# A two-layer hybrid decoder trunk whose opening is written in another order: x loaded first, squares summed in threes, bias indicators off GpSimd

## The chip, the core and the metric

The kernel runs on one core of a Trainium2 chip. Time is device time in microseconds (us) of one execution; the time of a kernel is the median of its runs. The core's engines each work through their own queue in order: TensorE (PE in the profile; its weight loads are PEld), VectorE (DVE), ScalarE (ACT) and GpSimd (POOL). Nearly all transfers are issued from SyncE's queue (SP), also in order.

## The reference

Two layers (DEPTH 2) over 512 tokens of width 2048. Each layer has a modulated RMS norm, one input projection into 7504 columns, sparse attention with an index scorer (top 128 keys, a T5 relative-position bias shared by both layers), retention with rotary, and one output projection:

```python
for l in range(DEPTH):
    mod = c_act @ w_mod[l] + b_mod[l]
    shift, scale, gate = jnp.split(mod, 3, axis=-1)
    h = rmsnorm(x, norm_gain[l]) * (1.0 + scale[:, None, :]) + shift[:, None, :]
    proj = h @ w_in[l]
    q_a, k_a, v_a, g_a, q_i, k_i, w_i, q_b, k_b, v_b, g_b = jnp.split(proj, split_points, axis=-1)
    q_a = rmsnorm(q_a.reshape(B, S, N_HEADS_A, HEAD_DIM), q_norm_gain[l])
    k_a = rmsnorm(k_a, k_norm_gain[l])
    att = sparse_attention(q_a, k_a, v_a, q_i.reshape(B, S, IDX_HEADS, IDX_DIM), k_i, w_i,
                           positions, rel_bias)
    y_a = att.reshape(B, S, D_A) * jax.nn.silu(g_a)
    q_b = rotary(q_b.reshape(B, S, N_HEADS_B, HEAD_DIM), positions)
    k_b = rotary(k_b.reshape(B, S, N_HEADS_B, HEAD_DIM), positions) * (HEAD_DIM ** -0.5)
    ret = retention(q_b, k_b, v_b.reshape(B, S, N_HEADS_B, HEAD_DIM))
    y_b = head_groupnorm(ret, ret_norm_gain[l]).astype(x.dtype) * jax.nn.silu(g_b)
    y = jnp.concatenate([y_a, y_b], axis=-1) @ w_out[l]
    x = x + gate[:, None, :] * y
```

The bias is `rel_bias[t5_bucket(pos_q - pos_k)]`, a table lookup per query, key and head; it does not depend on the layer's data.

## The kernel before, in words

Everything is held with features on the partitions: x and the normalised input h are 16 K-tiles of 128 features by 512 tokens. A projection is a product of fp32 numbers that are split into an upper and a lower fp32r half, so that each product is three matmuls (lines 330 to 332, or 336 to 338 for groups that are laid out by token): h upper with w upper, h lower with w upper, h upper with w lower. For the weights ScalarE writes the upper half (`wh`, line 268) and VectorE the lower (`wl`, line 275), each into a ring of three buffers; the loaded chunk `wf` has a ring of three too. `ahead` issues loads, upper and lower halves a chunk or two before the chunk's matmuls.

Work is a `stream` of chunks of groups. A group owns some columns of w_in, a few PSUM tiles and a function that evacuates them; a chunk is two to four K-tiles of it.

The opening, `start()`, is recorded by hand: each engine's queue has the instructions in the order in which Python issues them. It does five things.

1. It loads x and squares it on ScalarE; VectorE adds the squares, PE sums them over partitions (`row_sums`, line 511, tile `prs`), and `rstd_col` makes 1/rms and broadcasts it through PE (`prb`, line 493). `warm(n)` (line 476, tile `pw`) puts n small matmuls of zeros into PE's queue, whose result nobody reads.
2. It computes layer 0's modulation. Each K-tile needs a shift and a scale column, each one VectorE instruction over a 128 x 2048 piece of w_mod (1 MB) times the broadcast silu(c) (`mod_add`, line 357; the first four columns are done in two halves). In the text they are the adds. A K-tile of h then takes x times rstd (line 527, VectorE), the upper half (line 533, ScalarE), the same in fp32 (line 537 on ScalarE, or 535 on VectorE for the first tiles), and the lower half (line 539, VectorE).
3. Since K-tiles come one by one, PE is given early work, in the order of `PLAN`. `("S", c)` is chunk c (K-tiles 2c and 2c+1) of the group S, which holds the attention keys, values and index keys; `("S", 0, k)` is one K-tile of chunk 0. `("E", i, a, b)` is K-tiles a to b-1 of piece i, over 256 columns; pieces 0 to 3 are index queries (QI, 384 tokens), 4 to 7 are one retention head's query and key each (QB and KB, 512 tokens). A fourth number again means one K-tile alone. The result of a first piece is copied out by ScalarE (`part`, line 1257); later pieces of the same columns are added to it by VectorE (line 1272). The groups behind the opening start where PLAN stopped (`EARLY`) and join the stored part (line 1264).
4. The loop over `WORK` (PLAN with costs) decides how the rest is woven in: after each item its cost is added to `t`, and when `t` reaches RMOD one more add is issued (`mod_step`); if an item needs a K-tile that has not been issued, adds are forced first. In the same way a bias unit is issued for each RBIAS of cost, once KBIAS K-tiles are there.
5. The bias tables: 32 units. Each has four indicator tiles (positions against thresholds) and twelve bf16 matmuls with 32 columns of stationary operand (line 790, tile `pb`), a copy out of PSUM with an added column (`bt`, line 797) and a store to DRAM. Indicators are 0.5/-0.5 values by GpSimd (line 779, with doubled tables `be`) or signs by ScalarE (line 781). Seven units (`EU`, five of them on GpSimd) are issued by hand; `bias_tables` issues the rest, in the loop and then in the steady part.

PSUM has two tags of four banks: `pj` for S and all later groups, `px` for the early pieces E, the bias units, `warm` and the steady part's small products.

Behind the opening, `step` takes the stream chunk by chunk and `fill` runs tasks (index scores, top-k, rotary, retention, attention, bias) beside it; there the order is a scheduler's.

The lines that order the opening before:

```python
for k in range(KT):
    q = G("sq") if k else ssq
    act(q, X[k], AF.Square)
    ...
    if k % 3 == 0 and 0 < k < KT - 1:
        col = row_sums(pss, q, col)
        warm(WS if k < 12 else WL)
    elif k:
        tt(ssq, ssq, q, op=OP.add)
    if k < 3:
        mod0_add()
```

Of the kernel before, what the change touches and what calls it, by code (L numbers as in the profile page):

```python
# [45 lines left out]
PLAN = [("S", 0, 0), ("E", 0, 0, 2, 0), ("S", 0, 1), ("E", 0, 0, 2, 1), ("E", 1, 0, 2),  # L46
# [7 lines left out]
RBIAS, KBIAS = 6.0, 3  # L54
# [81 lines left out]
def hybrid_trunk(ctx, tc, xt, positions, wmod, w_in, w_out, cst_d, dec_d, out):  # L136
# [343 lines left out]
    def rstd_col(pss, n, then=None, tag="px"):  # L480
# [4 lines left out]
        if then:  # L485
            then()
        nc.vector.reciprocal(r, r)
# [55 lines left out]
    def start():  # L543
        rot, bias = rot_tables(), bias_tables()
        mod0_loads(4)
        for k in range(KT):
            load_x(k)
        ahead(1, 0)
        mod0_loads(6)
        ahead(2, 0)  # L550
# [32 lines left out]
        ssq, col, u = G("ssq"), 0, 0
        mod0_add()
        for k in range(KT):
            q = G("sq") if k else ssq
            act(q, X[k], AF.Square)
# [774 lines left out]
```

## Time and profile before

| | us |
|---|---|
| median of 3 runs (lowest, highest) | 1901.75 (1899.94, 1902.48) |
| the profiled execution, its own time | 1902.44 |
| its span | 1900.6 |
| PE busy, PEld busy | 1857.5, 1557.3 |
| DVE, ACT, POOL busy | 1300.0, 802.0, 90.6 |
| mean granted PE clock | 0.986 |

The profile is one execution. Matmuls are pipelined, so a busy PE is not PE at its peak; what counts is where it starts late or waits. The span is cut into 40 slices of 47.5 us for the overview; finer stretches come from the trace. A wait in brackets names the engine whose instruction ended it. Differences between kernels are taken from the profiled execution's own time (1902.44, of which 1900.6 is the span) and then applied to the median.

### The profile page before, as it was taken

The numbers are of one execution on the slowest core, as the hardware profiler recorded it, in microseconds if no ns is written. First come the engines' busy times: TensorE is split into PE (matmuls) and PEld (weight loads), VectorE is DVE, ScalarE is ACT, GpSimd is POOL, SyncE is SP. The second block draws the span as 40 slices with busy tenths as digits, with TensorE's granted clock in tenths as the row PEclk, the third lists the DMA queues.
The fourth block names the chain that finished last, engine by engine and source line by source line (L and its number), as shares of the span: only waits on it lengthen the run. The fifth ranks groups of instructions, "written<-read, shape, count | busy, mean of one in ns | idle before, by whom it ended". The sixth has DMA issues, their size and how long they took to land.

```text
span 1900.6 us, 24723 instructions
## 1 busy us (share of the span) xinstructions
PE 1857.5 (98%) x9124; PEld 1557.3 (82%) x9124; DVE 1300.0 (68%) x2254; ACT 802.0 (42%) x1480; POOL 90.6 (5%) x172
## 2 busy tenths in 40 slices
PE   6899999999999999999999999999999999999999
PEld 5687888888888888888889987888888888888887
DVE  7688599898767855777767689466775785564232
ACT  5665572355446532322225441245444554233211
POOL 8200000000000000100000000000000000000000
PEclk6899999999999999999999999999999999999999
DMA  9789423333353546789873333333334254653442
GB/s 341 283 301 294 132 60 89 100 111 105 99 183 114 178 143 202 241 268 309 293 258 105 101 87 97 108 95 100 105 102 131 74 189 133 189 180 119 144 142 102
DMA packets 166617, 304.43 MB, mean 160 GB/s; under 512 B 16352, under 2 KB 72416, under 8 KB 162912
## 3 DMA queue, kind: packets, MB, share of 16 engines
q1 hardware_dynamic: 166208, 302.37, 49.8%
q8 instruction: 71, 1.16, 0.2%
q10 hardware_dynamic: 288, 0.48, 0.1%
q14 instruction: 50, 0.41, 0.1%
HBM read 289.18 MB, written 13.63 MB: 159 GB/s over the span
## 4 chain that ended last, share of the span: by engine, by line
PE 82%; DVE 9%; ACT 4%; issue 2%; POOL 2%; DMA 2%; SPq 0%; DVEq 0%; ACTq 0%
PE pj L332 19%; PE pj L330 19%; PE pj L331 19%; PE pj L336 5%; PE pj L338 5%; PE pj L337 5%; DVE wl L275 2%; DVE mw L357 2%; POOL ind L779 2%; DVE iacc L928 1%; DVE m L927 1%; DVE iacc L913 1%; DMA xT<-in_xt_dram 1%; PE ptr L173 1%; ACT qsq L1075 1%
## 5 line engine op out<-in xcount | busy, mean ns | idle before, releaser
L275 DVE TENSOR_TENSOR wl<-wf,wh 128x1024 fp32r<-128x1024 f32 (+2 forms) x309 | 366.0, 1185 | 438.8 <-ACT wh L268 427.0
L268 ACT ACTIVATE wh<-wf 128x1024 fp32r<-128x1024 f32 (+2 forms) x309 | 318.8, 1032 | 794.0 <-PE pj L331 567.7
L332 PE MATMUL pj<-h,wl 128*128 128x512 f32 (+1 forms) x1280 | 486.1, 380 | 4.3 <-DVE wl L275 4.3
L330 PE MATMUL pj<-h,wh 128*128 128x512 f32 (+1 forms) x1280 | 488.1, 381 | 0.7 <-DVE join L1264 0.7
L331 PE MATMUL pj<-h,wh 128*128 128x512 f32 (+1 forms) x1280 | 486.0, 380 | 0.4 <-DVE h L539 0.4
L332 PEld LDWEIGHTS pj<-h,wl 128*128 128x128 f32 x1280 | 240.4, 188 | 46.0 <-DVE wl L275 5.7
L330 PEld LDWEIGHTS pj<-h,wh 128*128 128x128 f32 x1280 | 240.5, 188 | 44.7 <-issue 3.5
L331 PEld LDWEIGHTS pj<-h,wh 128*128 128x128 f32 x1280 | 240.4, 188 | 39.8 <-DVE h L539 0.9
L336 PE MATMUL pj<-wh,h 128*128 128x512 f32 (+1 forms) x640 | 242.5, 380 | 2.6 <-DVE vm L943 2.5
L338 PE MATMUL pj<-wh,h 128*128 128x512 f32 (+1 forms) x640 | 240.8, 378 | 1.6 <-DVE h L539 1.6
L337 PE MATMUL pj<-wl,h 128*128 128x512 f32 (+1 forms) x640 | 241.8, 378 | 0.0
L332 PE MATMUL pj<-y,wl 128*128 128x512 f32 x512 | 199.3, 389 | 0.0
L331 PE MATMUL pj<-y,wh 128*128 128x512 f32 x512 | 199.3, 389 | 0.0
L330 PE MATMUL pj<-y,wh 128*128 128x512 f32 x512 | 199.3, 389 | 0.0
L336 PEld LDWEIGHTS pj<-wh,h 128*128 128x128 f32 x640 | 121.6, 190 | 25.9 <-ACT wh L268 3.3
L338 PEld LDWEIGHTS pj<-wh,h 128*128 128x128 f32 x640 | 121.2, 190 | 21.8 <-DVE h L539 1.8
L337 PEld LDWEIGHTS pj<-wl,h 128*128 128x128 f32 x640 | 121.6, 190 | 19.4 <-DVE wl L275 0.2
L330 PEld LDWEIGHTS pj<-y,wh 128*128 128x128 f32 x512 | 96.1, 188 | 20.2
L331 PEld LDWEIGHTS pj<-y,wh 128*128 128x128 f32 x512 | 96.1, 188 | 19.9
L332 PEld LDWEIGHTS pj<-y,wl 128*128 128x128 f32 x512 | 96.1, 188 | 19.8
L357 DVE CUSTOM_DVE_ANT_0 mw<-mw,cb 128x1024 f32<-128x1024 f32 (+1 forms) x64 | 93.0, 1453 | 7.3 <-POOL mp L356 5.6
L357 DVE CUSTOM_DVE_ANT_0 mw<-mw,cb,mp 128x1024 f32<-128x1024 f32 x68 | 89.2, 1311 | 12.6 <-POOL md L356 7.6
(442 smaller groups left out, 2167.5 us busy)
## 6 DMA issues: line engine op xcount, KB each, us to landing
wf<-in_w_in_dram SPq DMA_DIRECT2D x155, 512.0 KB, 3.6
mw<-in_wmod_dram SPq DMA_DIRECT2D x136, 512.0 KB, 5.7
wf<-in_w_in_dram SPq DMA_DIRECT2D x136, 256.0 KB, 3.1
wf<-in_w_out_dram SPq DMA_DIRECT2D x64, 512.0 KB, 4.1
mw<-in_wmod_dram SPq DMA_DIRECT2D x28, 1024.0 KB, 7.8
dec<-in_decay_dram SPq DMA_DIRECT2D x32, 256.0 KB, 4.1
xT<-in_xt_dram SPq DMA_DIRECT2D x16, 256.0 KB, 5.4
bias<-bias_d SPq DMA_DIRECT2D x16, 256.0 KB, 4.1
```

Of the source, the lines that this page charges most:

```text
L173: nc.tensor.transpose(o, i, idn)
L268: act(h[:, :n], wf[i][:, :n], AF.Copy)
L275: tt(lo[:, :n], wf.pop(i)[:, :n], f(whl[i][:, :n]), op=OP.subtract)
L330: mm(q, wh[:, o:o + P], ah, start=s0, stop=False)
L331: mm(q, wh[:, o:o + P], al, start=False, stop=False)
L332: mm(q, wl[:, o:o + P], ah, start=False, stop=s1)
L336: mm(q, ah[:, n * P:(n + 1) * P], wh[:, o:o + g.N], start=s0, stop=False)
L337: mm(q, ah[:, n * P:(n + 1) * P], wl[:, o:o + g.N], start=False, stop=False)
L338: mm(q, al[:, n * P:(n + 1) * P], wh[:, o:o + g.N], start=False, stop=s1)
L357: nc.vector.tensor_tensor_reduce(w[:, lo:hi], w[:, lo:hi], cb[:, lo:hi], scale=ng(l, k, 1) if q == 1 else 1.0, scalar=init, op0=OP.mult, o ...
L779: nc.gpsimd.tensor_scalar(v, tab["pos"][:, :w], tab["pt"][:, col:col + 1], 0.5, op0=OP.is_lt, op1=OP.subtract)
L913: stt(a[:, :w], r[:, :w], L["WI"][:, c0:c0 + 1], a[:, :w], op0=OP.mult, op1=OP.add)
```

## The change

Four things are rewritten in `start()` and its helpers.

- x is loaded ahead of w_mod: eleven tiles, the first weight chunk, five tiles, and then w_mod. Squares are added up in threes (`SUMS`), and each sum goes to PE by itself. The adds of K-tile 0 come behind the root and no longer between the squares. K-tile 0's h is made as the others are. ScalarE's table for the root is loaded at the very start.
- Three bias units are issued by hand in place of seven: two with indicators on VectorE (before the squares and at K-tile 6), one on ScalarE (behind the last square). GpSimd makes only the small tables. All three units' matmuls stand behind the broadcast of 1/rms, with 24 `warm` matmuls behind them.
- PLAN begins with S and the retention pieces 4 and 5 on K-tile 0 and again on K-tile 1; these two pieces come in three parts (tiles 0 and 1, 2 to 5, 6 to 11) in place of two (0 to 2, 3 to 11). The QI pieces 0 to 3 follow on tiles 0 and 1.
- Bias units of the loop begin at seven K-tiles (three before), one for each 7.0 of cost (6.0 before). In a forced step the lower half of the tile is issued at once.

The core of the diff:

```diff
@@ -43,25 +43,26 @@
...
-PLAN = [("S", 0, 0), ("E", 0, 0, 2, 0), ("S", 0, 1), ("E", 0, 0, 2, 1), ("E", 1, 0, 2),
-        ("E", 2, 0, 2), ("E", 3, 0, 2), ("E", 4, 0, 3), ("E", 5, 0, 3), ("S", 1), ("E", 6, 0, 4), ("E", 7, 0, 4),
-        ("E", 0, 2, 6), ("E", 1, 2, 6), ("S", 2), ("E", 2, 2, 8), ("E", 3, 2, 8), ("S", 3),
-        ("S", 4), ("E", 6, 4, 12), ("E", 7, 4, 12), ("S", 5), ("E", 4, 3, 12), ("E", 5, 3, 12), ("S", 6), ("S", 7)]
+PLAN = [("S", 0, 0), ("E", 4, 0, 2, 0), ("E", 5, 0, 2, 0), ("S", 0, 1), ("E", 4, 0, 2, 1), ("E", 5, 0, 2, 1),
+        ("E", 0, 0, 2), ("E", 1, 0, 2), ("E", 2, 0, 2), ("E", 3, 0, 2), ("E", 6, 0, 4), ("E", 7, 0, 4), ("S", 1),
+        ("E", 4, 2, 6), ("E", 5, 2, 6), ("E", 0, 2, 6), ("E", 1, 2, 6), ("S", 2), ("E", 2, 2, 8), ("E", 3, 2, 8), ("S", 3),
+        ("S", 4), ("E", 6, 4, 12), ("E", 7, 4, 12), ("S", 5), ("E", 4, 6, 12), ("E", 5, 6, 12), ("S", 6), ("S", 7)]
...
 RMOD = 4.0
-RBIAS, KBIAS = 6.0, 3
+RBIAS, KBIAS = 7.0, 7
...
-WA, WS, WL, WR = 24, 4, 20, 8
-
-EU = [1, 1, 0, 1, 0, 1, 1]
-EUK = (9,)
+WA, WS, WR, WL = 24, 10, 8, 24
+
+EUK = (-1, 6, KT)
+SUMS = (2, 5, 8, 11, 13, 14, 15)
+XW = 11
...
@@ -477,14 +478,13 @@
 
     HALF = (slice(0, T // 2), slice(T // 2, T))
 
-    def rstd_col(pss, n, then=None, tag="px"):
+    def rstd_col(pss, n, tag="px", fill=0):
 
         r = sm("rcol", NB)
         nc.vector.tensor_reduce(r, pss[:, :n].rearrange("p (k j) -> p j k", j=NB), axis=AX.X, op=OP.add)
         act(r, r, AF.Sqrt, bias=eps, scale=1.0 / D)
-        if then:
-            then()
         nc.vector.reciprocal(r, r)
+        warm(fill)
         state["prb"] = []
         for c in HALF:
             pb = psum.tile([P, T], F32, name="prb", tag=tag)[:, c]
@@ -542,82 +542,78 @@
 
     def start():
         rot, bias = rot_tables(), bias_tables()
-        mod0_loads(4)
-        for k in range(KT):
+        for k in range(XW):
             load_x(k)
         ahead(1, 0)
+        for k in range(XW, KT):
+            load_x(k)
+        mod0_loads(4)
+        ahead(2, 0)
         mod0_loads(6)
-        ahead(2, 0)
+        ahead(3, 0)
         mod0_loads(8)
-        ahead(3, 0)
         warm(WA)
         act(cs, cst[:, C_C:C_C + KT], AF.Silu)
+        act(sm("dummy", 1), cs[:, :1], AF.Sqrt, bias=eps, scale=0.0)
         pos_tables()
         pc = [bcast_c(i) for i in range(4)]
+        inds = {}
+
+        def early(k):
+            if k in EUK:
+                u = len(inds)
+                inds[u] = indicators(*UNITS[u], k < KT)
+
+        early(-1)
         for i in range(4):
             v = cb[:, i * T:(i + 1) * T]
             if i % 2:
                 nc.vector.tensor_copy(v, pc[i])
             else:
                 act(v, pc[i], AF.Copy)
+
+        pss = psum.tile([P, T], F32, name="prs", tag="pj")
+        col, acc = 0, None
+        for k in range(KT):
+            q = G("sq")
+            act(q, X[k], AF.Square)
+            if acc is None:
+                acc = q
+            else:
+                tt(acc, acc, q, op=OP.add)
+            if k in SUMS:
+                col = row_sums(pss, acc, col)
+                acc = None
+                warm(WS if k < KT - 3 else 0)
+            early(k)
+            if k == XW:
+                ahead(1, 1)
+        early(KT)
+        rstd_col(pss, col, tag="pj", fill=WR)
+        units = [unit_mm(*UNITS[u], inds[u], EUK[u] < KT) for u in range(len(EUK))]
+        warm(WL)
+        mod0_add()
+        mod0_add()
+        xr = {0: make_xr(0)}
+        copy_rstd()
+        for u in units[:2]:
+            unit_end(*u)
+        mod0_add()
+        mod0_add()
+        h0 = make_h0(0, xr.pop(0))
+        next(h0)
+        next(h0)
+        for u in units[2:]:
+            unit_end(*u)
         act(onesr, ones, AF.Copy)
-        ind = {}
-
-        def get_ind(n):
-            for u in range(len(ind), min(n, len(EU))):
-                ind[u] = indicators(*UNITS[u], EU[u])
-
-        pend = []
-
-        def begin(u):
-            get_ind(u + 1)
-            pend.append(unit_mm(*UNITS[u], ind[u], EU[u]))
-
-        def flush(n=0):
-            while len(pend) > n:
-                unit_end(*pend.pop(0))
-
-        get_ind(2)
-
-        pss = psum.tile([P, T], F32, name="prs", tag="pj")
-        ssq, col, u = G("ssq"), 0, 0
-        mod0_add()
-        for k in range(KT):
-            q = G("sq") if k else ssq
-            act(q, X[k], AF.Square)
-            if k == KT // 2:
-                act(sm("dummy", 1), cs[:, :1], AF.Sqrt, bias=eps, scale=0.0)
-            if k % 3 == 0 and 0 < k < KT - 1:
-                col = row_sums(pss, q, col)
-                warm(WS if k < 12 else WL)
-            elif k:
-                tt(ssq, ssq, q, op=OP.add)
-            if k < 3:
-                mod0_add()
-            if k in EUK:
-                flush()
-                begin(u)
-                u += 1
-        flush()
-        col = row_sums(pss, ssq, col)
-        warm(WR)
-        rstd_col(pss, col, lambda: ahead(3, 0, 1), "pj")
-        ahead(3, 1)
-        begin(u)
-        u += 1
-        make_h(0, 0, X[0], state["prb"])
-        copy_rstd()
-        ahead(3, 2)
-        flush()
-        get_ind(u + 3)
-        st.update(have=0, t=RMOD, tb=0.0, done=0)
-        hgen, xr = {}, {}
+        st.update(have=1, t=0.0, tb=0.0, done=0)
+        hgen = {}
 
         def get_xr(k):
             if k < KT and k not in xr:
                 xr[k] = make_xr(k)
 
-        def mod_step():
+        def mod_step(now=False):
 
             if m0["add"] < len(steps0):
                 b, lo, hi = steps0[m0["add"]]
@@ -632,22 +628,17 @@
             if end:
                 hgen[k] = make_h0(k, xr.pop(k))
                 next(hgen[k])
+                if now:
+                    next(hgen.pop(k))
+                    st["have"] = k + 1
             return size
 
-        st["have"] = 1
-        ahead(5, 2)
         late, after = [], None
         for i, only, kend, cost in WORK:
             while st["have"] < kend:
                 if DEBUG:
                     print("forced", i, st["have"], kend)
-                mod_step()
-            if kend == 2:
-                for u in range(u, len(EU)):
-                    begin(u)
-                    flush(1)
-                flush()
-                u = len(EU)
+                st["t"] -= RMOD * mod_step(True)
             end = only is None or only == stream[i][0].kper - 1
             ahead(max(st["done"] + 3, i + 1), max(st["done"] + 1, i + 1))
             chunk_mm(i, only, late)
@@ -775,19 +767,19 @@
...
-                if pool:
-                    nc.gpsimd.tensor_scalar(v, tab["pos"][:, :w], tab["pt"][:, col:col + 1], 0.5, op0=OP.is_lt, op1=OP.subtract)
+                if dve:
+                    ts(v, tab["pos"][:, :w], tab["pt"][:, col:col + 1], 0.5, op0=OP.is_lt, op1=OP.subtract)
                 else:
                     act(v, tab["pos"][:, :w], AF.Sign, bias=tab["pt"][:, col:col + 1], scale=-1.0)
...
-    def unit_mm(j, q, ind, pool=False):
+    def unit_mm(j, q, ind, dve=False):
...
-                mm(ps[32 * tau:32 * tau + 32, :w], tab["parts"][pool][i], ind[tau],
+                mm(ps[32 * tau:32 * tau + 32, :w], tab["parts"][dve][i], ind[tau],
...
```

The remaining hunks move the small tables of `pos_tables` from VectorE to GpSimd and its four position differences `pt` from GpSimd to VectorE.

In what order the engines now find their work shows at three places. First VectorE, behind the shift and scale columns of K-tile 1. Before (hv, h and xT are K-tiles; mw the w_mod pieces; md the columns):

```order
L535 TENSOR_SCALAR hv_489<-xT_112,md0_90 128x512
L357 ISA mw0_254,md0_90<-mw0_254,cb_87 128x2048
L357 ISA md0_90 128x1
L539 TENSOR_TENSOR h_413<-hv_489,h_413 128x512
L527 TENSOR_TENSOR xT_114<-xT_114,rstd_420 128x512
L357 ISA mw0_266,md0_90<-mw0_266,cb_87,cst_74 128x2048
L357 ISA md0_90 128x1
L361 TENSOR_TENSOR md0_90<-md0_90,mb0_92 128x2
L275 TENSOR_TENSOR wl_621<-wf_153,wh_595 128x512
L275 TENSOR_TENSOR wl_646<-wf_447,wh_616 128x512
```

Now (h_479 is K-tiles 0 and 1; wl_585, wl_610, wl_638 and wl_663 are the lower weight halves of QI pieces 0 to 3; mw0_461 is the first piece of w_mod for K-tile 2):

```order
L535 TENSOR_SCALAR hv_541<-xT_106,md0_90 128x512
L539 TENSOR_TENSOR h_479<-hv_541,h_479 128x512
L276 TENSOR_TENSOR wl_585<-wf_557,wh_567 128x512
L276 TENSOR_TENSOR wl_610<-wf_559,wh_581 128x512
L358 ISA mw0_461,md0_90<-mw0_461,cb_87 128x2048
L358 ISA md0_90 128x1
L276 TENSOR_TENSOR wl_638<-wf_569,wh_605 128x512
L276 TENSOR_TENSOR wl_663<-wf_583,wh_630 128x512
L527 TENSOR_TENSOR xT_108<-xT_108,rstd_465 128x512
```

The lower halves of QI pieces 0 and 1 now stand ahead of the first add for K-tile 2, where before both adds for K-tile 2 came ahead of the next two lower halves.

Second, ScalarE, at the same time. Before, where the first lower halves' upper halves are written:

```order
L268 ACTIVATE wh_595<-wf_153 128x512
L533 ACTIVATE h_602<-xT_114,md0_90 128x512
L537 ACTIVATE xT_114<-xT_114,md0_90 128x512
L268 ACTIVATE wh_616<-wf_447 128x512
L1257 ACTIVATE part_623<-pj0_471 128x384
L1257 ACTIVATE part_625<-pj1_472 128x384
```

Now (part_571 and part_573 evacuate retention piece 4 from its PSUM tiles, part_587 and part_589 piece 5; wh_567, wh_581 and wh_605 are the upper halves of QI pieces 0, 1 and 2):

```order
L533 ACTIVATE h_479<-xT_106,md0_90 128x512
L269 ACTIVATE wh_567<-wf_557 128x512
L1249 ACTIVATE part_571<-pj0_509 128x512
L1249 ACTIVATE part_573<-pj1_510 128x512
L269 ACTIVATE wh_581<-wf_559 128x512
L1249 ACTIVATE part_587<-pj0_521 128x512
L1249 ACTIVATE part_589<-pj1_522 128x512
L269 ACTIVATE wh_605<-wf_569 128x512
```

The upper half of QI piece 1 now stands behind the copies of retention piece 4, which can run only when PE has finished that piece on K-tile 1.

Third, VectorE behind K-tile 5. Before (h_804 on xT_120 is K-tile 5, xT_122 K-tile 6):

```order
L539 TENSOR_TENSOR h_804<-xT_120,h_804 128x512
L275 TENSOR_TENSOR wl_990<-wf_807,wh_893 128x1024
L527 TENSOR_TENSOR xT_122<-xT_122,rstd_420 128x512
L357 ISA mw0_802,md0_90<-mw0_802,cb_87,cst_74 128x2048
L357 ISA md0_90 128x1
L361 TENSOR_TENSOR md0_90<-md0_90,mb0_92 128x2
L275 TENSOR_TENSOR wl_1037<-wf_861,wh_963 128x1024
L1272 TENSOR_TENSOR part_623<-pj0_999,part_623 128x384
L1272 TENSOR_TENSOR part_625<-pj1_1000,part_625 128x384
L357 ISA mw0_915,md0_90<-mw0_915,cb_87 128x2048
```

Now (h_821 on xT_114 is K-tile 5; pj0_840 to pj1_876 are the PSUM tiles of retention pieces 4 and 5 on K-tiles 2 to 5):

```order
L539 TENSOR_TENSOR h_821<-xT_114,h_821 128x512
L276 TENSOR_TENSOR wl_871<-wf_742,wh_814 128x1024
L1264 TENSOR_TENSOR part_571<-pj0_840,part_571 128x512
L1264 TENSOR_TENSOR part_573<-pj1_841,part_573 128x512
L276 TENSOR_TENSOR wl_905<-wf_782,wh_866 128x1024
L1264 TENSOR_TENSOR part_587<-pj0_875,part_587 128x512
L1264 TENSOR_TENSOR part_589<-pj1_876,part_589 128x512
L358 ISA mw0_780,md0_90<-mw0_780,cb_87 128x2048
```

Before, both adds for K-tile 6 stood ahead of any sum (mw0_802 is the second; the first is just above these rows), and two sums of a QI piece followed. Now four sums of the retention pieces, which need PE's results, stand ahead of the first add for K-tile 6 (mw0_780).

More of the change, by code (lines that the diff above doesn't have):

```diff
@@ L743, in pos_tables @@
         for tl in range(4):
-            nc.gpsimd.tensor_scalar(pt[32 * tl:32 * tl + 32, :], p4[32 * tl:32 * tl + 32, tl, :],
+            ts(pt[32 * tl:32 * tl + 32, :], p4[32 * tl:32 * tl + 32, tl, :],
                                     cst[32 * tl:32 * tl + 32, C_THR:C_THR + 1], None, op0=OP.subtract)
+        pts, ptt = nc.gpsimd.tensor_scalar, nc.gpsimd.tensor_tensor
         top = sm("top", 1)
-        ts(top, cst[:, C_TOP:C_TOP + 1], 0.5, None, op0=OP.mult)
+        pts(top, cst[:, C_TOP:C_TOP + 1], 0.5, None, op0=OP.mult)
         bd = sm("bd", 32)
         rb = sm("rb", HA)
-        tt(rb, cst[:, C_RB:C_RB + HA], cst[:, C_RS:C_RS + HA], op=OP.subtract)
+        ptt(rb, cst[:, C_RB:C_RB + HA], cst[:, C_RS:C_RS + HA], op=OP.subtract)
         for tl in range(4):
-            ts(bd[:, tl * HA:(tl + 1) * HA], rb, cst[:, C_BLK + tl:C_BLK + tl + 1], 0.5,
+            pts(bd[:, tl * HA:(tl + 1) * HA], rb, cst[:, C_BLK + tl:C_BLK + tl + 1], 0.5,
                op0=OP.mult, op1=OP.mult)
@@ L757, in pos_tables @@
             b = sm(f"bd{i}", 32, dt=BF)
-            nc.vector.tensor_copy(b, bd)
+            nc.gpsimd.tensor_copy(b, bd)
             if i < 2:
-                tt(bd, bd, b, op=OP.subtract)
+                ptt(bd, bd, b, op=OP.subtract)
             parts.append(b)
             b2 = sm(f"be{i}", 32, dt=BF)
-            nc.gpsimd.tensor_scalar(b2, b, 2.0, None, op0=OP.mult)
+            pts(b2, b, 2.0, None, op0=OP.mult)
             twice.append(b2)
@@ L767, in hybrid_trunk, with indicators @@
     UNITS = [(j, q) for j in reversed(range(NB)) for q in range(8)]
-    def indicators(j, q, pool=False):
+    def indicators(j, q, dve=False):
         w = P * (j + 1)
@@ L803, in bias_tables @@
     def bias_tables():
-        todo = UNITS[len(EU):]
+        todo = UNITS[len(EUK):]
         nxt = indicators(*todo[0])
```

## The prediction, made before the result was known

> **What bounds the kernel now.** I read the page's slices first, then the busy time by stretches, then the chain of waits of the first 61 us. TensorE (PE) is full from the third slice to the end, so time is lost only in the opening.
>
> ```profile
> PE   6899999999999999999999999999999999999999
> POOL 8200000000000000100000000000000000000000
> PEclk6899999999999999999999999999999999999999
> 33.70:37.60 3.90, 3.90 (x26) 3.64 (x26) 3.29 (x5) 3.90 (x9) 3.90 (x3) 0.79 0.49 127
> 37.60:59.80 22.20, 8.53 (x62) 2.16 (x61) 11.48 (x16) 5.70 (x9) 20.77 (x9) 0.60 0.69 262
> 59.80:134.30 74.50, 70.28 (x432) 60.05 (x431) 63.42 (x80) 58.80 (x98) 0.00 (x0) 0.98 0.88 305
> 134.30:137.70 3.40, 3.39 (x12) 3.39 (x13) 3.09 (x5) 1.55 (x5) 0.00 (x0) 0.50 1.04 390
> 137.70:206.00 68.30, 66.15 (x418) 52.04 (x417) 51.04 (x69) 40.31 (x83) 0.00 (x0) 1.00 0.81 263
> 206.00:1900.60 1694.60, 1680.62 (x8020) 1414.73 (x8020) 1146.79 (x2035) 675.03 (x1254) 38.92 (x140) 1.00 0.46 144
> ...
> 27.91 30.47 POOL ind L779 x13
> ```
>
> Rows with a colon: stretch, length, busy time of PE, PEld, DVE, ACT, POOL, PE's granted clock, DMA. The reader sees four things. Projection work starts at 33.70. From 37.60 to 59.80 PE does only five bias units and waits, and the chain says for what: GpSimd's indicators. From 59.80 until the early work ends at 206 PE is nearly full. Behind 206 it is busy 1680.62 of 1694.60 us, so nothing is to be had there: the change is worth what it moves before 206, less what it pushes behind it.
>
> **The start.** These rows carry the first projection matmul, at 33.70:
>
> ```profile
> 11.99 0.63 ACT L587 ACTIVATE ssq<-xT 128x512 f32<-128x512 f32 x1 [4.11 <-DMA xT<-in_xt_dram]
> 12.66 5.37 ACT L587 ACTIVATE sq<-xT 128x512 f32<-128x512 f32 x8
> 20.21 1.87 PE L511 MATMUL prs<-cst,sq 128*128 128x1 f32 x8 [1.14 <-ACT sq L587]
> 22.46 1.47 PE L790 MATMUL pb<-ind,be 128*32 128x512 bf16 x12
> 25.59 2.29 PE L476 MATMUL pw<-wz 128*128 128x128 bf16 x20
> 30.07 0.18 DVE L487 RECIPROCAL rcol<-rcol 128x4 f32<-128x4 f32 x1 [0.36 <-ACT rcol L484]
> 30.30 2.08 PE L493 MATMUL prb<-cst,rcol 128*128 128x128 f32 x8
> 33.70 0.65 PE L336 MATMUL pj<-wh,h 128*128 128x336 f32 x1
> 34.96 5.00 ACT L781 ACTIVATE ind<-pos,pt 128x512 bf16<-128x512 f32 x8
> 37.92 1.28 DVE L357 CUSTOM_DVE_ANT_0 mw<-mw,cb,cst 128x1024 f32<-128x1024 f32 x1
> 41.60 0.93 DVE L535 TENSOR_SCALAR hv<-xT,md 128x512 f32<-128x512 f32 x1
> ...
> 211.56 0.43 DVE L712 TENSOR_SCALAR nn<-ang 128x512 f32<-128x512 f32 x1 [0.42 <-PE pka L173]
> ```
>
> x tiles land 0.67 us apart (5.37/8), the first at 12.0 behind four w_mod pieces of 512 KB; at that pace these are 5.4 us, so x begins at 6.6 and ends, with the first weight chunk inside, at 17.5. But VectorE (DVE) now has two bias units' indicators there. Their form stands nowhere on DVE; the nearest rows are a tensor_scalar of 0.43 (0.46 with its gap) and the 0.93 of the one beside GpSimd, so eight cost 3.7 to 7.4 us. I take 0.46, since GpSimd is quiet then. From 8.0 (positions cast and subtracted) DVE has 1.8 of indicators, 1.2 of copies, four sums of 0.61, 1.8 of indicators, four sums, the first lower half (0.78) and the last sum: 19.0. Only then can PE add up groups 13, 14 and 15: 2.8 us at full clock, 5.6 at half (1.87 each). With reduce, root and reciprocal 22.5 (25.3 at half) where 30.07 stood. ScalarE's four indicators ahead of the root (2.5 us, 5.00/2) end at 20.6 and stay hidden; if DVE were quick they would set it. Four half adds of 1.21, the scaled x (0.8) and one ScalarE pass make 7.0 more: projection starts at **29.5**. At half clock PE has row 2.08, three bias units of 1.47 and 24 fillers of 0.115 after the reciprocal, so 34.7. I take 29.5, since ten fillers behind each sum keep PE occupied: gain **4.2**, with ends -1.0 and 5.5 (ScalarE setting the root). The w_mod pieces now stand behind x in SP's queue: at 1.3 each they land from 18.9 to 22.9, and DVE takes them from 22.7 on, so that costs nothing unless the start comes 4 us sooner.
>
> **The gap.** 22.2 us go. Seven units stood ahead of the full stretch, now three; four more meet a busy PE:
>
> ```profile
> 76.25 0.76 PE pb L790 x12
> 77.01 0.43 PE pj L330
> 77.44 0.23 PE pj L331
> ...
> PE pj L332 <- DVE wl L275: 4.3, 3, 1.7
> PE pj L338 <- DVE h L539: 1.6, 1, 1.6
> PE pj L331 <- DVE h L539: 0.4, 1, 0.4
> ```
>
> One costs 0.76 + 0.43 - 0.23 = 0.96, four 3.8. The old plan's own stops between 59.8 and 206 go too: 6.3 by the wait rows, and what half clock cost there: 0.79 over 3.90 means 1.6 us at half, 0.98 over 74.5 means 2.9, and 3.4 more at 0.50: 7.9, of which half, 3.9, is lost. (Only the first of these three lies ahead of 59.8, in the old S on tile 0.) The old early work would so be ready 32.8 us sooner.
>
> **What is late next.** The K-tiles. In the gap DVE got ahead; without it PE asks for each tile as DVE makes it. Prices:
>
> ```profile
> L357 DVE CUSTOM_DVE_ANT_0 mw<-mw,cb,cst 128x2048 f32<-128x2048 f32 x13 | 30.5, 2345 | 0.0
> L357 DVE CUSTOM_DVE_ANT_0 mw<-mw,cb 128x2048 f32<-128x2048 f32 x13 | 29.7, 2283 | 0.0
> L275 DVE TENSOR_TENSOR wl<-wf,wh 128x1024 fp32r<-128x1024 f32 x10 | 12.2, 1222 | 3.0 <-ACT wh L268 2.7 <-issue 0.3
> L539 DVE TENSOR_TENSOR h<-xT,h 128x512 fp32r<-128x512 f32 x14 | 9.6, 687 | 3.5 <-ACT xT L537 3.5
> L527 DVE TENSOR_TENSOR xT<-xT,rstd 128x512 f32<-128x512 f32 x13 | 8.9, 682 | 0.0
> L1272 DVE TENSOR_TENSOR part<-pj,part 128x512 f32<-128x512 f32 x8 | 5.3, 686 | 8.4 <-PE pj L332 8.4
> L537 ACT ACTIVATE xT<-xT,md 128x512 f32<-128x512 f32 x14 | 11.4, 816 | 0.5
> L533 ACT ACTIVATE h<-xT,md 128x512 fp32r<-128x512 f32 x14 | 11.3, 808 | 9.9 <-DVE md L361 9.9
> ```
>
> Start to start these are 0.08 less. A K-tile costs DVE two adds with bias (4.7), xT and h (1.2): 5.9, and each lower weight half 1.14 per 1024 columns beside it. PE's matmul takes 0.23 per 512 columns; shorter ones I estimate in proportion. I walked DVE, ScalarE and PE along the new queues; times run from the moment when tile 0 is whole (30.1).
>
> Tile 1: PE has S and two retention pieces on tile 0, 4.7 us; DVE needs 9.4. Stop 4.5. Tiles 2 and 3: DVE has 15.2 of work from tile 1 to tile 3, but stands 5.7 behind the lower half of QI piece 1, whose upper half waits on ScalarE behind the evacuation of the retention piece; and 1.9 for ScalarE's two passes on tile 3. Whole at 32.2; PE asks at 25.1 and 27.2. Stop 6.5. Tile 5: 14.8 of work and 3.8 of waits, whole at 50.7, PE asks at 47.3: 3.2. Tile 7: the sums of the retention pieces (part) now stand in DVE's queue ahead of the next add and wait for PE; whole at 80.0, PE idles 4.3. Tiles 9 and 11, in the same way: 4.1 and 3.7; later ones 0.5, since PE then has 35 us of work per pair. Together **26.8**. The DMA is not the bound: x (4.2 MB), twelve w_mod tiles of 1.05, weights and the rest (5) are 22 MB up to tile 5, at the 390 GB/s of the row at 134.30 there by 62; DVE asks at 76.
>
> The stop that ends at 134.3 was 1.6 us by its row, and the clock was 0.50 for the next 3.40. Three stops here add up to over 4; half clock costs up to 1.7 each (half of 3.40), and I count half of it, since the stream is partly waiting then: **2.6**, with ends 0 and 10.2 (six stops at full price). [...]
>
> **Sum**, against the execution's own 1902.44: 4.2 + 22.2 - 3.8 + 6.3 + 3.9 - 26.8 - 2.6 = 3.4 us faster, 1899.0. The three runs shown have their median 0.7 lower: **1898.4**. Under 0.2% (3.8 us) a measurement of this kernel can't tell from no change, so this stands close to that bound.
>
> **Rivals.** *Supply keeps its old pace.*
>
> ```profile
> 64.48 2.28 DVE L357 CUSTOM_DVE_ANT_0 mw<-mw,cb 128x2048 f32<-128x2048 f32 x1
> 175.02 2.35 DVE L357 CUSTOM_DVE_ANT_0 mw<-mw,cb,cst 128x2048 f32<-128x2048 f32 x1
> 180.14 0.69 DVE L539 TENSOR_TENSOR h<-xT,h 128x512 fp32r<-128x512 f32 x1 [1.66 <-ACT xT L537]
> ...
> PE pb L790 <- ACT ind L781: 1.9, 1, 1.9
> ```
>
> Before, 25 adds took 110.5 us (8.8 a tile, my walk 10.4). If that holds from the seventh full-tile add, at 54.0, the last starts at 164.5, tile 15 is whole at 169.6 and the early work ends at 173 against 206; 13 bias units are left behind it, 25 done before and 12 now (four of 384 columns, eight of 256, one of 128): 7.0 in proportion to columns, 12.5 at full price, I take 9. So 24 faster, **1877.7**. For it: DVE is busy only 63.42 of 74.50 before, with waits on PE in it already. Against it: the sums in front of the adds. Chance 0.25.
>
> *The bias units left over stall PE* (slower). Twenty instead of seven run behind the early work, beside index scores that use the same PSUM tag and ScalarE. Of seven, one waited 1.9 us for its indicator (last row above). If each of the 13 does, 24.7: **1923**; every second, 1911. Two such waits use up my gain, four make it slower by over 0.2%. Chance 0.12.
>
> *The start doesn't come.* PE falls to half clock before the root: 34.7. That loses 5.2, and tile 1's stop shrinks by 2.7: **1900.9**. Before, the clock was half from before 22.46 on in just this place. Chance 0.18.
>
> **How the numbers follow.** The forecast has 0.45: of it 0.20 faster, 0.20 within 0.2%, 0.05 slower. The first rival is faster; the second slower 0.10, same 0.02; the third same 0.13, slower 0.05. Faster 0.45, same 0.35, slower 0.20. The range takes in half clock at full price (7.6 more: 1906), one end of the start (5.2 more), and most of the first rival: 1880 to 1907; the forecast's own is 1892 to 1905.
>
> **What would show it.** First projection matmul near 29.5; no wait on GpSimd; PE waits on h at tiles 1, 3, 5, 7, 9, 11 of some 27 us in all; DVE waiting on PE at part; the last early S matmul near 191; 20 bias units behind it without waits. I am wrong if the waits on h are under 15 us, if S starts after 33, or if PE is less than 99% busy behind the early work.

## The result, and the profile after

| | us |
|---|---|
| median of 4 runs (lowest, highest) | 1919.27 (1917.19, 1921.66) |
| the kernel before beside it, median of 4 runs | 1901.37 |
| ratio, 95% interval | 1.0095 [1.0077, 1.0112] |
| span of the profiled execution; mean granted PE clock | 1917.4; 0.983 |

The changed kernel is slower by 17.9 us, outside the predicted range of 1880 to 1907.

The page's slices of the changed kernel, one digit for 48 us, busy tenths:

```profile
PE   8789999999999999999999999999999999999999
POOL 1000000000000000100000000000000000000000
PEclk7899999999999999999999999999999999999999
```

GpSimd is out of the opening, as intended, and PE is still not full in the first three slices. The time can be split at the first projection matmul (S on tile 0). These are stretches of the changed kernel and of the kernel before, from that matmul to the end: length, then busy time of PE, PEld, DVE, ACT, POOL, granted clock, DMA.

```profile
36.23:1917.40 1881.17, 1842.32 (x8945) 1542.98 (x8944) 1281.34 (x2210) 789.29 (x1458) 39.32 (x140) 0.99 0.49 155
33.70:1900.60 1866.90, 1832.87 (x8960) 1536.02 (x8956) 1279.10 (x2206) 785.29 (x1452) 63.59 (x151) 0.99 0.49 157
```

S starts 2.5 later; behind it PE is idle 38.85 us where it was 34.03 (1881.17 - 1842.32; 1866.90 - 1832.87), 4.8 more; and it is busy 9.45 longer with nearly the same work. Together 16.8, the difference of the spans. Most of the busy part is clock. These are the stretches of the changed kernel behind S in which the clock was 0.50, and then those of the kernel before, with the same columns:

```profile
44.16:50.98 6.82, 5.55 (x17) 4.93 (x18) 2.27 (x6) 1.78 (x3) 0.00 (x0) 0.50 0.33 115
64.64:78.29 13.65, 8.14 (x17) 5.25 (x18) 9.80 (x12) 5.65 (x9) 0.00 (x0) 0.50 0.80 267
122.66:129.49 6.83, 6.23 (x19) 6.24 (x20) 4.27 (x6) 2.63 (x5) 0.00 (x0) 0.50 0.94 285
143.14:149.97 6.83, 5.69 (x19) 5.27 (x20) 5.51 (x6) 2.20 (x3) 0.00 (x0) 0.50 0.36 106
208.00:214.82 6.82, 5.96 (x22) 5.54 (x22) 4.68 (x15) 3.94 (x13) 0.00 (x0) 0.50 0.82 264
245.54:248.96 3.42, 3.37 (x12) 3.37 (x13) 3.25 (x7) 2.09 (x4) 0.00 (x0) 0.50 0.63 202
...
42.14:62.62 20.48, 9.87 (x46) 4.33 (x46) 7.71 (x9) 5.42 (x9) 16.23 (x7) 0.50 0.56 224
134.30:137.72 3.42, 3.41 (x12) 3.41 (x13) 3.11 (x5) 1.57 (x5) 0.00 (x0) 0.50 1.03 388
994.50:997.90 3.40, 3.40 (x26) 3.34 (x24) 1.40 (x4) 0.92 (x2) 0.00 (x0) 0.50 0.08 21
```

PE is busy for 34.94 us at half clock now. Before it was 16.68 by these rows, and 1.62 more at the start of S, from 33.70 to 35.32. Half of each counts as lost, 17.5 against 9.2, an estimate from the clock of 0.50 (the changed kernel's matmuls of 512 columns start 0.43 us apart from 49.12 on, at 0.50, and 0.23 from 39.98 on, at 1.00), and the 8.3 between them is most of the longer busy time. The waits of PE on K-tiles and weight halves in the first 215 us (total, times, longest):

```profile
PE pj L331 <- ACT h L533: 9.4, 4, 3.3
PE pj L337 <- ACT h L533: 8.2, 3, 3.9
PE pj L332 <- DVE h L539: 5.4, 5, 1.7
PE pj L339 <- DVE h L539: 1.5, 2, 0.9
PE pj L333 <- DVE wl L276: 1.2, 2, 0.8
PE pj L338 <- DVE wl L276: 0.9, 2, 0.5
```

They add up to 26.6. So the gap of 22.2 us is gone, and stops on K-tiles and half clock have taken its place. The question is why the K-tiles come late: the last one's lower half, the last row of line 539, starts at 208.5, and before it started at 180.1 (the changed kernel's row first; first and last start in the line; the 14 are K-tiles 2 to 15):

```profile
L539 DVE TENSOR_TENSOR h<-xT,h x14: 686/692/693, 66.7 to 208.5; 128x512 fp32r<-128x512 f32 x14
L539 DVE TENSOR_TENSOR h<-xT,h x14: 683/686/693, 66.7 to 180.1; 128x512 fp32r<-128x512 f32 x14
```

### The profile page after: what moved, and what is told of

Same layout as the page of the kernel before. It is cut to its first block, busy times and chain, and to the rows that moved or that the text cites. A ratio compares the mean times of both kernels' runs of the same rounds, so it can differ in the third digit from the quotient of the medians.

```text
span 1917.4 us, 24819 instructions
## 1 busy us (share of the span) xinstructions
PE 1873.3 (98%) x9172; PEld 1571.1 (82%) x9172; DVE 1301.3 (68%) x2257; ACT 808.3 (42%) x1491; POOL 44.7 (2%) x159
## 4 chain that ended last, share of the span: by engine, by line
PE 83%; DVE 9%; ACT 5%; DMA 2%; issue 1%; SPq 0%; ACTq 0%; POOL 0%; DVEq 0%
PE pj L332 19%; PE pj L331 19%; PE pj L333 19%; PE pj L337 5%; PE pj L339 5%; PE pj L338 5%; DVE mw L358 2%; DVE wl L276 2%; DVE iacc L920 1%; DVE m L919 1%; PE pdot L897 1%; DMA wf<-in_w_in_dram 1%; DVE iacc L905 1%; PE prs L511 1%; PE ptr L174 1%
## 5 line engine op out<-in xcount | busy, mean ns | idle before, releaser
L276 DVE TENSOR_TENSOR wl<-wf,wh 128x1024 fp32r<-128x1024 f32 (+3 forms) x309 | 365.8, 1185 | 429.4 <-ACT wh L269 422.3
L269 ACT ACTIVATE wh<-wf 128x1024 fp32r<-128x1024 f32 (+3 forms) x309 | 318.7, 1032 | 798.7 <-PE pj L332 580.4
L332 PEld LDWEIGHTS pj<-y,wh 128*128 128x128 f32 x512 | 96.1, 188 | 20.1
```

The costliest lines, as they stand in the source:

```text
L269: act(h[:, :n], wf[i][:, :n], AF.Copy)
L276: tt(lo[:, :n], wf.pop(i)[:, :n], f(whl[i][:, :n]), op=OP.subtract)
L332: mm(q, wh[:, o:o + P], al, start=False, stop=False)
```

## The experiments

A ratio below is to the kernel before, with its 95% interval, from runs on the same chip. In the changed kernel's loop one line stands out that the list of the change does not name: a forced addition (an add of a w_mod piece that PE's next work needs and that has not been issued) is now charged to the pace, `st["t"] -= RMOD * mod_step(True)`. Each takes RMOD, 4 us of PE's work, off `t`, so the following additions are issued only when PE's work has paid for it. It is called the debit here.

**The gap alone.** The kernel before, with GpSimd's indicators made by DVE:

```diff
-                    nc.gpsimd.tensor_scalar(v, tab["pos"][:, :w], ...
+                    ts(v, tab["pos"][:, :w], ...
```

> The kernel before with one thing changed: the five units whose indicators GpSimd made get them from DVE (0.42 us each, 1.7 per unit); order of loads, early groups, additions and bias pacing stay. Theory A (the changed kernel lost its gain to the order of its queues: additions behind weight halves, K-tile 0's additions behind the root, a late start): with the old order kept, most of the 22.2 us gap is won, less some 8.5 us of indicators on DVE: 1886 to 1893, and the waits on h up to 210 us stay under 12 us. Theory B (the gap only covered the making of the K-tiles, whatever the order): the waits on h take it back, over 18 us of them, and the time is 1898 to 1905.

Measured 1890.75, ratio 0.9945 [0.9929, 0.9962]; the waits on h and on lower weight halves are 8.1 us in the first 215 (6.3 in the kernel before):

```profile
PE pj L332 <- DVE wl L275: 4.8, 4, 1.8
PE pj L338 <- DVE h L539: 1.8, 1, 1.8
PE pj L331 <- DVE h L539: 1.5, 1, 1.5
```

Theory A holds: without the gap, in the old order, the K-tiles do come nearly in time. Theory B falls, and with it the prediction's reason for the stops.

**The order of the early groups.** The changed kernel with before's PLAN (its first line of four):

```diff
-PLAN = [("S", 0, 0), ("E", 4, 0, 2, 0), ("E", 5, 0, 2, 0), ("S", 0, 1), ...
+PLAN = [("S", 0, 0), ("E", 0, 0, 2, 0), ("S", 0, 1), ("E", 0, 0, 2, 1), ...
```

> The changed kernel with the early groups' order of before (PLAN alone). The two retention groups then ask for K-tiles 0 and 1 in the old order and there are 17 matmul groups fewer on K-tile 0. Theory A1 (the new order of groups starves PE): 8 to 15 us faster than the changed kernel, 1904 to 1911. Theory A2 (the order of additions and weight halves on DVE and the late start do it, the groups' order does not): within 4 us of 1919, or slower, since there is less work per K-tile.

1928.40, 1.0139 [1.0124, 1.0154]: 9 us slower than the changed kernel. A1 was wrong, the new order helps there.

**The fillers.** None behind the sums:

```diff
-WA, WS, WR, WL = 24, 10, 8, 24
+WA, WS, WR, WL = 24, 0, 8, 24
```

> The changed kernel without the ten filler matmuls behind each of four sums (WS = 0). Theory A (sums and fillers are a queue at half clock from 13 to 28.7 us, each group of ten fillers costs 1.23): S on tile 0 starts 2.5 to 4 us sooner (near 33), the time is 2 to 4 us less, 1915 to 1917. Rival (the fillers keep PE at a higher clock, as the prediction had it): the half clock lasts longer or PE waits, S starts no sooner than 36.2 and the time is 1919 or more.

1915.04, 1.0068 [1.0053, 1.0083], 4.2 us less; S on tile 0 starts at 33.84 instead of 36.23. PE's queue around the root with the fillers, and without them:

```profile
20.74 1.81 PE L511 MATMUL prs<-cst,sq 128*128 128x1 f32 x8
22.41 1.23 PE L477 MATMUL pw<-wz 128*128 128x128 bf16 x10
23.43 5.23 PE L511 MATMUL prs<-cst,sq 128*128 128x1 f32 x24
28.52 1.01 PE L477 MATMUL pw<-wz 128*128 128x128 bf16 x8
...
19.73 6.54 PE L511 MATMUL prs<-cst,sq 128*128 128x1 f32 x30
26.14 1.01 PE L477 MATMUL pw<-wz 128*128 128x128 bf16 x8
```

DVE's last sum of squares is there at 20.1 and 20.3. With fillers PE is through the sums at 28.5, without them at 26.1.

**The pacing, whole and in half.** Both lines of it back, then the debit alone:

```diff
-        st.update(have=1, t=0.0, tb=0.0, done=0)
+        st.update(have=1, t=RMOD, tb=0.0, done=0)
...
-                st["t"] -= RMOD * mod_step(True)
+                mod_step(True)
```

> The changed kernel with the pacing of before: forced additions are not charged to the pace (t stays) and the pace starts with one addition due. Additions then stand some places earlier in DVE's queue, ahead of weight halves and part sums. Theory A (order in DVE's queue): 4 to 10 us faster, 1909 to 1915, waits on h down from 24.5 us by as much. Rival (DVE and ScalarE as a whole, or the weight loads, set the pace): within 3 us of 1919.

1896.59, 0.9975 [0.9965, 0.9985]: 22.7 us less than the changed kernel, more than theory A had.

> The changed kernel with one half of the pacing edit undone: forced additions are no longer charged to the pace, which still starts at 0. Theory A (each stop's additions were charged, so the next ones were emitted too late and the next stop came: the debit feeds itself): nearly all of the 22.7 us that the whole old pacing won, 1895 to 1901. Rival (the starting value, one addition earlier at tile 1, sets off the rest): under a third of it, 1912 to 1919.

1895.49, 0.9967 [0.9956, 0.9978]. The debit is all of it; the starting value has no effect that these runs show. PE's waits without the debit in the first 215 us, its busy time from S on tile 0 to the end, and the row of line 539:

```profile
PE pj L337 <- ACT h L533: 4.3, 2, 3.9
PE pj L333 <- DVE wl L276: 4.1, 2, 3.7
PE pj L331 <- ACT h L533: 2.0, 1, 2.0
PE pj L332 <- DVE h L539: 1.7, 2, 1.1
...
36.85:1895.40 1858.55, 1832.81 (x8944) 1537.94 (x8944) 1280.97 (x2210) 788.47 (x1458) 38.93 (x140) 0.99 0.50 157
L539 DVE TENSOR_TENSOR h<-xT,h x14: 684/686/693, 57.4 to 174.8; 128x512 fp32r<-128x512 f32 x14
```

One line of Python, and the last K-tile's lower half starts 33.7 us sooner (174.8 against 208.5). With two smaller rows (0.7 and 0.2) the waits are 13.0 where they were 26.6, so about half of the stops stay. Behind S, PE is idle for 25.7 us instead of 38.9 and busy for 9.5 less, although S starts no sooner (36.85). What the line does in DVE's queue shows in DVE's own waits, with the debit and without it:

```profile
DVE h L539 <- ACT xT L537: 17.4, 8, 3.6
DVE part L1264 <- PE pj L333: 16.9, 11, 2.3
...
DVE part L1264 <- PE pj L333: 10.1, 7, 3.1
DVE h L539 <- ACT xT L537: 2.6, 2, 1.7
```

With it, DVE stands at sums of retention pieces that wait for PE (16.9), with additions behind them that PE is about to wait for; and a forced K-tile is made start to finish in one go, so that DVE waits for ScalarE's pass (17.4), where an early one has the next addition in between. One wait of DVE moves the other way: that of the lower weight halves on the upper ones is 6.9 with the debit and 14.9 without, so the three together fall from 41.2 to 27.6. The program's own count of forced additions while it writes the queues is twelve with the debit and five without it.

**The debit without the rest.** The same two lines put into the kernel without the gap, and into the kernel before itself:

> The kernel before with indicators on DVE instead of GpSimd (1890.8) and, in addition, the changed kernel's pacing: forced additions are charged and the pace starts at 0. Theory A (the debit is harmful wherever PE has to force additions): 6 to 20 us slower than 1890.8, 1897 to 1911, with waits on h. Rival (the debit only hurts with two retention groups on K-tile 0): within 3 us of 1890.8.

1920.21, 1.0101 [1.0086, 1.0116]: 29.5 us over 1890.75, more than the 20 that theory A had at most.

> The kernel before, GpSimd's indicators kept, with the changed kernel's pacing alone (forced additions charged, pace from 0). Theory (the debit feeds itself wherever PE forces an addition, gap or not): 10 to 35 us slower than before, 1911 to 1937. Rival (in the gap DVE gets far enough ahead that no addition is forced): within 4 us of 1901.5.

1929.50, 1.0145 [1.0130, 1.0161]: 27.6 over the kernel before beside it (1901.87). In both the count of forced additions is 24, and five without the two lines. The three pairs (in the changed kernel the debit alone, in the other two both lines):

| | without the debit | with it |
|---|---|---|
| before, GpSimd's gap kept | 1901.87 | 1929.50 |
| before, indicators on DVE | 1890.75 | 1920.21 |
| the changed kernel | 1895.49 | 1919.27 |

**Half clock.** Fillers in PE's queue ahead of each of the nine forced additions behind K-tile 1, 24 and then 16:

```diff
             while st["have"] < kend:
+                warm(16 if kend > 2 else 0)
                 st["t"] -= RMOD * mod_step(True)
```

> The changed kernel with 24 filler matmuls in PE's queue ahead of each of the nine forced additions behind K-tile 1: the stops stay, PE is no longer idle in most of them. It tells what half clock costs apart from the stops. If half clock behind these stops costs 8 to 12 us (busy time of PE behind S on tile 0 is 9.5 us over before's): 5 to 9 us faster, 1910 to 1914, and under 15 us of half clock from 60 to 260 us where there were 34. If it costs 2.6 us, as the prediction had it, or the fillers only delay the next matmuls: within 3 us of 1919, or slower.

1918.65, 1.0090 [1.0073, 1.0107]: no gain.

> The changed kernel with 16 instead of 24 fillers ahead of each forced addition behind K-tile 1 (24 gave 1918.65, no gain, but no undisturbed profile). If half clock behind the stops costs nothing because the K-tiles set the pace: 1917 to 1920 again, half clock from 60 to 260 us under 20 us, the K-tiles whole at the same times as without fillers within 2 us. If 24 were only too many and half clock costs 8 us or more: 1911 to 1915.

1914.88, 1.0068 [1.0052, 1.0083], 4.4 less, at the upper end of the second answer's range. Behind S the clock was at half in these stretches only (their ends are 0.1 us off, hence 0.51 and 0.52):

```profile
44.89:51.72 6.83, 5.79 (x18) 5.14 (x19) 2.07 (x4) 2.02 (x3) 0.00 (x0) 0.51 0.29 101
68.79:79.03 10.24, 6.57 (x15) 4.83 (x16) 8.48 (x10) 2.88 (x4) 0.00 (x0) 0.51 0.80 256
143.88:147.30 3.42, 3.42 (x14) 3.42 (x13) 3.42 (x4) 0.00 (x0) 0.00 (x0) 0.52 0.48 119
1007.40:1010.86 3.46, 3.46 (x28) 3.40 (x26) 1.22 (x4) 0.55 (x2) 0.00 (x0) 0.52 0.14 36
```

PE is busy 19.24 at half clock instead of 34.94, 7.9 us less lost, and the time falls by 4.4. Up to K-tile 7, which is whole at 123.6 (123.2 in the changed kernel), little changed: 12.36 us of busy PE at half clock instead of 13.69. Behind it 3.42 are left of 21.25, beside a new stretch at 1007, and K-tile 15's lower half starts 2.5 us sooner (206.1). Whether the rest of the 7.9 went into the fillers' own time or into waits on K-tiles was not tried.

**The start.** On the kernel with the old pacing and no fillers, K-tile 0's additions ahead of the reduce (DVE's step that adds up PE's sums, with root and reciprocal behind it); then four groups of sums instead of seven; then also two additions behind the reciprocal and the three bias units in the stop at tile 1. The edit of the first two (`units[:2]` are the copies of the bias units):

```diff
+        for _ in range(4):
+            mod0_add()
         rstd_col(pss, col, tag="pj", fill=WR)
...
-SUMS = (2, 5, 8, 11, 13, 14, 15)
+SUMS = (5, 11, 14, 15)
...
-        for u in units[:2]:
-            unit_end(*u)
         h0 = make_h0(0, xr.pop(0))
```

> The changed kernel with the old pacing and without the ten fillers behind the sums. Theory A (the backlog of sums and fillers at half clock and the debit are separate losses): their gains add up, 22.7 + 4.2, 1891 to 1894, with S on tile 0 near 33.9. Rival (once the additions come early, an earlier start only lengthens the stop at tile 1): 1895 to 1898.

1893.56, 0.9963 [0.9950, 0.9976], S at 34.1: inside theory A's range. The gain over the same kernel with fillers is 1.9 to 3.0 us (1895.49 and 1896.59), less than the 4.2 that were to add up, and the intervals overlap.

> The changed kernel with the old pacing, no fillers behind the sums (1893.6), and in addition K-tile 0's four additions ahead of the reduce in DVE's queue, where DVE waits 6.0 us for PE's sums, and 8 instead of 24 fillers behind the units. Theory (the additions behind the root set the start): S on tile 0 from 34.1 to 31.3 to 32.3, the time 1 to 3 us less, 1890.5 to 1892.5. Rival (DVE still needs 9 us for K-tile 1, the stop there grows by what the start wins): 1893 to 1895.

1894.62, 0.9959 [0.9947, 0.9972], S at 33.85: no gain, and the start did not move, so neither answer was tested. PE's last forty sums end at 27.0, the last 33 of them 0.22 us each, as at 0.50 in the changed kernel (24 in 5.23), and ScalarE's pass for K-tile 0 stood behind its copies of the bias units.

> As h1_adds_before_root (1894.6, S on tile 0 at 33.85), with four groups of sums instead of seven (24 fewer N = 1 matmuls, three more additions of squares on DVE), no fillers behind the units, and ScalarE's pass for K-tile 0 ahead of its evacuations of the units. Theory (PE's sums, 1.81 us per eight at half clock, saturate PE from 18 to 26 and set the root): S on tile 0 at 30 to 32, and if a microsecond of start is worth one, 1891 to 1893. Rival (the stop at tile 1 takes it back): S starts sooner but the time stays at 1893.5 to 1895. Third (something else holds the start): S at 33 or later.

1893.38, 0.9954 [0.9942, 0.9967], S at 34.67, later: the third answer. Now PE waits for DVE, whose three more sums of squares and four additions hold the reduce until 28.2:

```profile
26.75 1.34 DVE L358 CUSTOM_DVE_ANT_0 mw<-mw,cb,mp 128x1024 f32<-128x1024 f32 x1
...
28.22 0.17 DVE L484 TENSOR_REDUCE rcol<-prs 128x4 f32<-128x16 f32 x1
```

> The changed kernel with the old pacing, before's order of early groups and no fillers behind the sums (1892.4), with four groups of sums, two of K-tile 0's additions ahead of the reduce and two behind the reciprocal, and the three early bias units moved from ahead of S on tile 0 into the stop at tile 1. Theory (PE's sums, DVE's additions and the units together held the start): S on tile 0 at 30 to 31.5, the time 2 to 4 us less, 1888 to 1890.5. Rival (K-tile 1's additions and the weight halves follow in DVE's queue as before, so the stop at tile 1 grows): S starts at 30 to 31.5 and the time stays within 1.5 us of 1892.4.

1893.47, 0.9949 [0.9936, 0.9962], S at 33.70, set by the two additions behind the reciprocal. No version started S before 33.5. Sums, additions and units each hold it near 34 when the others are out of the way; whether 29.5 can be had, and what it would be worth, stays open.

**The rest of the parts.** Before's order of groups (on the kernel of 1893.56), before's pacing of bias units (on the one of 1895.49), and all parts together:

```diff
-RBIAS, KBIAS = 7.0, 7
+RBIAS, KBIAS = 6.0, 3
```

> The changed kernel with the old pacing, no fillers (1893.6), and the early groups in before's order. Theory (the new order gives PE work while the K-tiles are made; under the debit it was worth 9 us): 3 to 9 us slower, 1897 to 1903. Rival (it only helped because the debit starved PE; without the debit the K-tiles come in time either way): within 2 us of 1893.6.

1892.38, 0.9950 [0.9937, 0.9962], against 0.9963 with the new order: the rival. Two groups on K-tile 0 only helped while the debit starved PE.

> The changed kernel without the debit (1895.5), and with the bias units paced as before (one per 6.0 from K-tile 3 on, instead of one per 7.0 from K-tile 7 on): some eight to twelve units move from behind the early work into it. Theory (left-over units cost behind what they cost in front, no waits): within 2 us of 1895.5. Rival (left over they stall PE): 2 to 8 us faster. Third (in front they crowd ScalarE and delay the K-tiles): 2 to 6 us slower.

1893.02, 0.9954 [0.9942, 0.9967], against 0.9967 [0.9956, 0.9978] with 20 units left over: the intervals overlap, and it decides little.

> As i1_fewer_sums, with the early groups in before's order (1892.4 against 1893.6 without the debit) and the bias units paced as before (1893.0 against 1895.5). If the parts add up: 1887 to 1890, faster than before's kernel without GpSimd indicators (1890.8). If they all remove the same loss: 1890 to 1893.

1891.50, 0.9946 [0.9933, 0.9958]. The parts do not add up. No version is clearly faster than the kernel before with one edit, indicators on DVE (0.9945). That one beats the kernel before and the changed kernel; its interval and that of all parts together overlap.

## Why the prediction was wrong

**What was right.** The gap went, DVE's indicators took the time assumed (0.42 us each, 0.46 assumed), and behind the early work the left-over bias units did not stall PE (from 215 to 420 us two waits):

```profile
PE pb L782 <- ACT ind L773: 1.5, 2, 1.3
```

The stops came to 26.6 where 26.8 was forecast. At K-tiles 1, 3, 5, 7, 9, 11 and behind they were 3.9, 7.5, 3.2, 3.3, 3.7, 2.4 and 2.6 (forecast 4.5, 6.5, 3.2, 4.3, 4.1, 3.7 and 0.5). Some luck is in the total, since K-tiles and PE both came later than in the walk. Two of the signs that the prediction named speak against it: S started after 33, and the last early S matmul came at 214.5 instead of near 191.

**The books.** In the split of the result the prediction reads as follows (its gap and its old stops and units sorted into idle and busy: 26.8 - 13.7 - 6.3, with 13.7 = 22.20 - 8.53; and 3.8 + 2.6 - 8.5 - 3.9):

| | forecast | measured |
|---|---|---|
| S on tile 0 starts | 4.2 sooner | 2.5 later |
| PE idle behind it | +6.8 | +4.8 |
| PE busy behind it | -6.0 | +9.5 |
| sum | -3.4 | +16.8 |

**First failed term: half clock, "2.6, with ends 0 and 10.2".** It came to 17.5, half of the 34.94 us measured at half clock. The prediction took the one stretch of 3.40 us in the old trace as the length of each, counted three of them, and at half price; here there are six, four of them 6.8 long and one 13.65. The debit is only part of this term: with it the clock is at half for 44.4 us behind S, without it still for some 21 (an estimate from that run's mean clocks, 0.989 over its span of 1895.4 and 0.72 over the 36.85 up to S), and up to half of that is lost. Not all of it need be a price, since the run with 16 fillers lost 7.9 less and won 4.4.

**Second failed term: the start, "since ten fillers behind each sum keep PE occupied: gain 4.2".** They kept PE occupied and not at full clock. It was at 0.50 from 13.4 to 33.9, and a PE that is occupied at half clock is a queue: a group of eight sums and ten fillers took 2.7 us. DVE's last sum of squares was there at 20.1, but four such groups kept PE from the last three groups of sums until 23.43. These took 5.2 and put the root at 28.9 and the reciprocal at 29.25, against 25.3 by the prediction's own half-clock end, which counted only the three last groups. From the reciprocal to S it took 7.0, as forecast.

**Third, the walk behind K-tile 1.** It had K-tile 3 whole 32.2 and K-tile 7 80.0 behind K-tile 0; the rows give 36.0 and 86.3:

```profile
36.20 0.69 DVE L539 TENSOR_TENSOR h<-hv,h 128x512 fp32r<-128x512 f32 x1 [0.30 <-ACT h L533]
72.21 0.69 DVE L539 TENSOR_TENSOR h<-xT,h 128x512 fp32r<-128x512 f32 x1 [1.73 <-ACT xT L537]
122.51 0.69 DVE L539 TENSOR_TENSOR h<-xT,h 128x512 fp32r<-128x512 f32 x1
...
64.08 1.06 ACT L269 ACTIVATE wh<-wf 128x1024 fp32r<-128x1024 f32 x1 [4.38 <-DMA wf<-in_w_in_dram]
65.05 0.80 ACT L533 ACTIVATE h<-xT,md 128x512 fp32r<-128x512 f32 x1
```

K-tile 2's upper half stood 4.38 us behind a weight that had not landed. "The DMA is not the bound" counted bytes and overlooked that a load can be issued late, since its buffer comes free only when DVE has made a lower half from it: SyncE's loads of weights waited 102.0 us for lower halves in the first 215, 29 times. This one was issued from 56.25 on, behind a lower half that ended at 56.22, and had landed at 64.01, behind 1 MB of w_mod that was issued at 54.40 and landed at 62.27.

**The reason was wrong where the number was right.** "In the gap DVE got ahead; without it PE asks for each tile as DVE makes it": the run of the gap alone refutes this, with 8.1 us of such waits and 10.9 us won. About half of the stops came from the debit (13.0 of 26.6 stay without it), which costs 24 to 30 us in all three kernels, gap or no gap. The prediction walked the queues that the debit had made, so it got its stops, and never asked which edit had made them. Of its rivals, the supply did not keep its old pace and the left-over units did not stall PE. The third, that the start doesn't come, did happen: PE was at half clock before the root, and S started even later than its 34.7. But its price, which gave 1900.9, is a fraction of the loss.

## What to carry to other kernels

Split a large change into its edits before sizing them, and give a line of pacing arithmetic the same suspicion as an engine swap: a debit for work that was issued too late makes the next work late too, and here it cost more than all other edits won. An engine kept busy with fillers is a queue for whatever comes behind (here DVE's last sum of squares was there at 20.1, and PE came to the last three groups of sums at 23.43), so count everything that stands in it at the clock that the trace shows. A stop costs its own length and, as behind six stops here, half clock of 3.4 to 13.7 us behind it, whose length is read from stretches like the new ones, half busy and half waiting, and not from a single short one.

## What the runs showed of the hardware

In this trace every change of the clock between 1.00 and 0.50 lies on one grid of 3.41 us: the start and end of the half clock before S, 13.44 and 33.92, lie nine and three steps ahead of 44.16, and the twelve ends of the six stretches in the result lie whole multiples of 3.413 us apart (from 44.16 to 248.96 it is 60 times 3.413). Stretches of that grid in the changed kernel's trace, and ten us of the time before S (busy PE is the second number, granted clock the third from the end):

```profile
119.25:122.66 3.41, 1.56 (x8) 0.92 (x6) 3.38 (x7) 2.37 (x3) 0.00 (x0) 1.00 0.90 330
122.66:126.07 3.41, 2.81 (x9) 2.82 (x10) 1.97 (x3) 0.00 (x0) 0.00 (x0) 0.50 0.92 255
126.07:129.49 3.42, 3.42 (x12) 3.42 (x11) 2.31 (x3) 2.63 (x5) 0.00 (x0) 0.50 0.95 314
88.53:91.94 3.41, 1.57 (x7) 0.94 (x6) 2.73 (x4) 0.61 (x1) 0.00 (x0) 1.00 0.78 324
91.94:95.35 3.41, 2.09 (x8) 1.49 (x9) 2.33 (x3) 1.96 (x3) 0.00 (x0) 1.00 0.00 0
20.00:30.00 10.00, 10.00 (x61) 9.79 (x60) 1.02 (x4) 1.19 (x3) 0.00 (x0) 0.50 1.06 395
```

Behind a stretch with PE busy for 1.56 us the clock fell; a stretch busy for 2.81 did not bring it back, the next, full one did. So four of the six stops behind which the clock fell ended inside a stretch at 0.50, and PE spent the rest of it and a whole one more at 0.50 (the four rows of 6.8 us in the result). It is no sharp rule: behind the stretch from 88.53, with 1.57 us busy, the clock stayed up. And a full PE is not always enough: from 20 to 30 it was busy all the time with sums of one column and fillers, at 0.50. In the kernel before, the clock even fell behind such work: PE was busy for all of 991.05 to 994.46, and the next stretch was at 0.50.
